# Decays of a bidirectional state-space scan: one minimum over both directions, or each direction by itself

## The chip, the cores and the metric

The kernel runs on one core of one Trainium2 chip. The metric is the device time of one execution in microseconds (us).

## The reference

The program is one layer of a bidirectional encoder trunk in float32 on 256 tokens of width 2048: a Mamba-2 scan in both directions, a 4-head cross-attention into 256 memory tokens, a gated feed-forward block with a convolution, and norms between them. What matters here is the scan. Its 64 heads of 64 features lie in 8 groups of 8 heads; a group shares one B and one C with 128 states. Time is cut into two chunks of 128 tokens. For one direction, with `cum` the running sum of `dt * A` (A is negative):

```
seg = exp(where(tril, cum[l] - cum[m], -inf))
cb  = C[l] . B[m]
y_diag[l] = sum over m of  cb[l,m] * seg[l,m] * dt[m] * x[m]
```

The backward direction is the same on flipped tokens, with `dt`, A and `cum` of its own, and both results are added. So a token pair (l, m) with m before l takes the forward decay and weight, a pair with m after l the backward one, and the diagonal takes both.

## The kernel before, in words

All matrix products with weights are made of float32 split in two parts: ACT copies a raw weight tile to `w_hi` (L106), DVE subtracts to get `w_lo` (L107), and PE multiplies hi by hi, hi by lo and lo by hi (L152, L153, L154 in `gemm_feat`, 24 matmuls to a weight tile of 128x1024 in the scan stage, 8 of each line). Raw tiles have a ring of 5 buffers (loaded by SP, L115), `w_hi` and `w_lo` a ring of 4 each.

The scan stage goes over 8 groups. For group g the program first writes down the projection of group g+1 (`project`: the products for x, then for B and C, each with the convolution and Silu), then the gate of group g (`project_z`), then `scan_group(g)`. Tile's planner places these instructions on the engines at build time, each engine's list in a fixed order, so the matmuls of the next projection stand between the steps of a group's scan.

The setup ahead of it (L296 to L356) computes `dt`, its transpose `dt_tok` (tokens in partitions), the running sums `cumT` for both directions, which go to `cum_d` in DRAM (L334), and `ncum_tok`, the negated running sums with tokens in partitions (L346). Exp, Ln and Silu need a table load on ACT when the function before was of another table.

`scan_group` takes both chunks c in turn. `r` (L423, one buffer, 128x2048) gets from `cum_d` the running sums of the group's 8 heads in both directions, sent to all 128 partitions (L424, 1 MB). `cb` holds C.B twice, masked for the forward and for the backward triangle (L428). Then:

- for each head: ACT adds the head's negated forward sum to the forward `r` (L435), DVE adds the negated backward sum to the backward `r` and takes the minimum of both (L436). One of the two is negative and the other positive off the diagonal, so the minimum is the right decay's exponent on either side;
- one Exp over all 8 heads (L438);
- for each head: ACT scales the backward `cb` by the backward `dt` (L441), DVE adds the forward `cb` times the forward `dt` (L442);
- DVE multiplies both (L444) to `t2`, and PE multiplies `t2` with x (L453). DVE adds the skip term and the part from the other chunk (L456 to L460), and in the end the gate (L464).

After the second chunk the same buffer `r` is loaded for the next group. SP works its list in order: L424 waits until `r` has been read, with the raw weight loads behind it.

Of the kernel before, what the change touches and what calls it, by code (L numbers as in the profile page):

```python
# [10 lines left out]
AF = mybir.ActivationFunctionType  # L11
ALU = mybir.AluOpType
AX = mybir.AxisListType

P = 128
T = 256
# [20 lines left out]
def kernel(  # L37
# [15 lines left out]
    nc = tc.nc  # L53

    const = ctx.enter_context(tc.tile_pool(name="const", bufs=1))
# [7 lines left out]
    def sb(pool, shape, tag, dtype=F32, **kw):  # L63
        return pool.tile(shape, dtype, tag=tag, name=tag, **kw)
# [178 lines left out]
    with tc.tile_pool(name="xin", bufs=1) as xin:  # L243
        xt = [sb(xin, [P, D], f"x{tt}") for tt in range(2)]
        dt_w = []
        for q4 in range(4):
            if q4 == 2:
                dt_w.append(load_raw(w_in_v, 0, [(10240, P)]))
            for tt in range(2):
                nc.sync.dma_start(out=xt[tt][:, q4 * 512:(q4 + 1) * 512],  # L250
                                    in_=x[tt * P:(tt + 1) * P, q4 * 512:(q4 + 1) * 512])
        ss = sb(xin, [P, 2, 4], "x_ss")
        for u in range(4):
            stage = sb(xin, [P, 4, T], "x_stage", bufs=2)
            for jj in range(2):
                ps = psum_m()
# [20 lines left out]
        ps = psum_m()  # L277
# [4 lines left out]
        nc.vector.tensor_copy(out=r_mix, in_=ps[:, :T])  # L282

    dt_tok = sb(const, [P, 2, P], "dt_tok")
    ncum_tok = sb(const, [P, 2, P], "ncum_tok")
    dx_tok = sb(const, [P, 2, 64], "dx_tok")
    units_y = []

    with tc.tile_pool(name="ssd", bufs=1) as ssd:
# [53 lines left out]
        ps = psum_m()  # L343
        for c in range(2):
            nc.tensor.transpose(out=ps[:, c * P:(c + 1) * P], in_=cumT[:, c, :], identity=ident)
        nc.vector.tensor_scalar(out=ncum_tok.rearrange("p c h -> p (c h)"), in0=ps[:, :T], scalar1=-1.0,  # L346
                                scalar2=None, op0=ALU.mult)

        ecum = pieces[10][:, :P]
        for c in range(2):  # L350
# [42 lines left out]
        def scan_group(g, xs, bc, sz):  # L393
            hs = slice(g * 8, (g + 1) * 8)
            er = sb(ssd, [P, 2, 4, P], "er")
            for q in range(2):
                for d in range(2):
                    nc.sync.dma_start(out=er[q * 64:(q + 1) * 64, d], in_=ecum_v[g, q, d].partition_broadcast(64))

            xs_tok = sb(ssd, [P, 2, 512], "xs_tok")  # L400
            xsd = sb(ssd, [P, 2, 512], "xsd")
            for c in range(2):
                ps = psum_m()
                for j in range(4):
                    nc.tensor.transpose(out=ps[:, j * P:(j + 1) * P], in_=xs[:, j, c * P:(c + 1) * P], identity=ident)  # L405
                nc.scalar.copy(out=xs_tok[:, c, :], in_=ps)
                nc.vector.tensor_tensor(out=xsd[:, c, :].rearrange("p (h f) -> p h f", f=64),
                                        in0=ps.rearrange("p (h f) -> p h f", f=64),
                                        in1=dx_tok[:, c, hs].unsqueeze(2).broadcast_to([P, 8, 64]), op=ALU.mult)
            b_tok = sb(ssd, [P, 2, P], "b_tok")  # L410
            ps = psum_m()
            for c in range(2):
                nc.tensor.transpose(out=ps[:, c * P:(c + 1) * P], in_=bc[:, 0, c * P:(c + 1) * P], identity=ident)
            nc.scalar.copy(out=b_tok.rearrange("p c n -> p (c n)"), in_=ps[:, :T])

            st = sb(ssd, [P, 2, 512], "st")
            for c in range(2):
                ps = psum_m()
                nc.tensor.matmul(ps, b_tok[:, c, :], xsd[:, c, :], start=True, stop=True)  # L419
                nc.scalar.copy(out=st[:, c, :], in_=ps)  # L420
            for c in range(2):
                cl = slice(c * P, (c + 1) * P)
                r = sb(ssd, [P, 2, 8, P], "r")  # L423
                nc.sync.dma_start(out=r, in_=cum_v[c, g].partition_broadcast(P))  # L424
                ps_cb = psum_m()
                nc.tensor.matmul(ps_cb[:, :P], bc[:, 0, cl], bc[:, 1, cl], start=True, stop=True)
                cb = sb(ssd, [P, 2, P], "cb")
                nc.vector.tensor_tensor(out=cb, in0=ps_cb[:, :P].unsqueeze(1).broadcast_to([P, 2, P]), in1=tri, op=ALU.mult)  # L428


                t1 = r[:, 0]
                t2 = sb(ssd, [P, 8, P], "t2", bufs=2)
                for h in range(8):
                    hf, hb = g * 8 + h, 64 + g * 8 + h
                    nc.scalar.activation(out=t1[:, h, :], in_=t1[:, h, :], func=AF.Identity, bias=ncum_tok[:, c, hf:hf + 1])  # L435
                    nc.vector.scalar_tensor_tensor(out=t1[:, h, :], in0=r[:, 1, h, :], scalar=ncum_tok[:, c, hb:hb + 1],  # L436
                                                   in1=t1[:, h, :], op0=ALU.add, op1=ALU.min)
                nc.scalar.activation(out=t1, in_=t1, func=AF.Exp)  # L438
                for h in range(8):
                    hf, hb = g * 8 + h, 64 + g * 8 + h  # L440
                    nc.scalar.activation(out=t2[:, h, :], in_=cb[:, 1, :], func=AF.Copy, scale=dt_tok[:, c, hb:hb + 1])  # L441
                    nc.vector.scalar_tensor_tensor(out=t2[:, h, :], in0=cb[:, 0, :], scalar=dt_tok[:, c, hf:hf + 1],  # L442
                                                   in1=t2[:, h, :], op0=ALU.mult, op1=ALU.add)
                nc.vector.tensor_tensor(out=t2, in0=t2, in1=t1, op=ALU.mult)  # L444

                ps_o = psum_m()
                for j in range(4):
                    nc.tensor.matmul(ps_o[:, j * P:(j + 1) * P], st[:, 1 - c, j * P:(j + 1) * P], bc[:, 1, cl],  # L448
                                     start=(j == 0), stop=(j == 3), skip_group_check=True)
                ps_y = psum_m()  # L450
                for h in range(8):
                    dst = ps_y[(h % 2) * 64:(h % 2 + 1) * 64, (h // 2) * P:(h // 2 + 1) * P]
                    nc.tensor.matmul(dst, xs_tok[:, c, h * 64:(h + 1) * 64], t2[:, h, :],  # L453
                                     start=(h < 2), stop=(h >= 6), skip_group_check=True)
                for j in range(4):
                    nc.vector.scalar_tensor_tensor(out=xs[:, j, cl], in0=xs[:, j, cl], scalar=pcol("dskip", g * 4 + j),  # L456
                                                   in1=ps_y[:, j * P:(j + 1) * P], op0=ALU.mult, op1=ALU.add)
                yo = er[:, 1 - c]
                nc.vector.tensor_tensor(out=yo, in0=ps_o.rearrange("p (j l) -> p j l", l=P), in1=yo, op=ALU.mult)
                nc.vector.tensor_tensor(out=xs[:, :, cl], in0=xs[:, :, cl], in1=yo, op=ALU.add)  # L460
            unit = new_unit()
            for b in range(2):
                bs = slice(2 * b, 2 * b + 2)
                nc.vector.tensor_tensor(out=xs[:, bs, :], in0=xs[:, bs, :], in1=sz[:, bs, :], op=ALU.mult)  # L464
                add_square(ssd, acc_y, xs[:, bs, :], g == 0 and b == 0)
                for j in range(2 * b, 2 * b + 2):
                    split_scaled(unit, j, xs[:, j, :], pcol("g_ssd", g * 4 + j))
            units_y.append(unit)
# [306 lines left out]
```

## Time and profile before

| what | us |
|---|---|
| median of 3 runs | 1862.79 (1862.3 to 1864.23) |
| the profiled execution | 1863.24 |
| its span, first to last instruction | 1861.5 |
| PE busy (matmuls) | 1842.3 |
| DVE busy | 1264.2 |
| ACT busy | 1018.2 |

PE is the matrix engine, PEld its weight loads, DVE the vector engine, ACT the scalar engine, SP the queue that issues the transfers. Busy time of PE is a union of matmuls whose ends are modelled. An instruction's duration can overlap the next one's on the same engine, so the pace of a row of equal instructions is read from their starts.

### The profile page before, as it was taken

The page shows a single profiled execution, that of the slowest core. Times are in us where ns is not written, and L with a number is a line of the kernel's source. Part 1 is how long each engine was busy: PE and PEld are TensorE (multiplying, and loading weights), DVE is VectorE, ACT ScalarE, POOL GpSimd, SP SyncE. Part 2 cuts the span into 40 slices and gives each one's busy share as a digit, 9 for nine tenths or more (in the row PEclk, how much of TensorE's full clock was granted, in tenths as well). Part 3 has the DMA queues.
Part 4 walks back from the last instruction along what each step waited for, and adds up shares of the span by engine and source line. Part 5 has one row for each costly group of instructions (what it writes and reads, how often), then busy time and mean ns, then how long its engine had stood idle before and what let it go on. Part 6 is the DMA issues. An engine that isn't in the chain of part 4 may idle for free.

```text
span 1861.5 us, 29854 instructions
## 1 busy us (share of the span) xinstructions
PE 1842.3 (99%) x11821; PEld 1663.5 (89%) x11821; DVE 1264.2 (68%) x1792; ACT 1018.2 (55%) x1454; POOL 2.3 (0%) x11
## 2 busy tenths in 40 slices
PE   8999999999999999999999999999999999999997
PEld 8999999999999988888888888888888888888886
DVE  6878888988887756655555667666664456666654
ACT  6667667766775645444444455555553345555443
POOL 0000000000000000000000000000000000000000
PEclk9999999999999999999999999999999999999999
DMA  8667666766766765655655556566666666666563
GB/s 289 198 203 214 199 189 201 219 197 201 215 182 205 244 197 182 184 177 170 176 176 181 164 187 206 179 189 188 191 191 192 193 192 188 185 187 187 190 193 114
DMA packets 289708, 358.94 MB, mean 193 GB/s; under 512 B 11616, under 2 KB 210656, under 8 KB 289056
## 3 DMA queue, kind: packets, MB, share of 16 engines
q1 hardware_dynamic: 289488, 356.76, 62.3%
q8 instruction: 92, 1.51, 0.3%
q14 instruction: 48, 0.39, 0.1%
q0 software_dynamic: 80, 0.28, 0.1%
HBM read 352.60 MB, written 4.39 MB: 192 GB/s over the span
## 4 chain that ended last, share of the span: by engine, by line
PE 99%; DMA 0%; DVE 0%; ACT 0%; SPq 0%; issue 0%; DVEq 0%
PE psg L169 30%; PE psg L171 16%; PE psg L154 10%; PE psg L153 10%; PE psg L152 10%; PE psm L194 6%; PE psm L193 6%; PE psm L195 6%; PE psm L453 1%; PE psm L448 1%; PE psm L419 1%; PE psm L589 0%; PE psm L591 0%; PE psm L590 0%; DMA x<-in_x_dram 0%; PE psm L405 0%
## 5 line engine op out<-in xcount | busy, mean ns | idle before, releaser
L107 DVE TENSOR_TENSOR w_lo<-raw,w_hi 128x1024 fp32r<-128x1024 f32 x618 | 753.7, 1223 | 499.3 <-ACT w_hi L106 497.1
L106 ACT CAST w_hi<-raw 128x1024 fp32r<-128x1024 f32 x618 | 645.7, 1049 | 684.0 <-PE psg L169 314.5
L169 PE MATMUL psg<-unit,w_hi 128*128 128x512 f32 x2432 | 853.3, 396 | 0.0
L171 PE MATMUL psg<-unit,w_lo 128*128 128x256 f32 x2432 | 683.4, 281 | 0.0
L169 PEld LDWEIGHTS psg<-unit,w_hi 128*128 128x128 f32 x2432 | 456.3, 188 | 106.0
L171 PEld LDWEIGHTS psg<-unit,w_lo 128*128 128x128 f32 x2432 | 460.7, 189 | 0.2
L154 PE MATMUL psg<-unit,w_lo 128*128 128x256 f32 x1552 | 444.8, 287 | 0.1
L152 PE MATMUL psg<-unit,w_hi 128*128 128x256 f32 x1552 | 442.4, 285 | 0.0
L153 PE MATMUL psg<-unit,w_hi 128*128 128x256 f32 x1552 | 441.6, 285 | 0.0
L154 PEld LDWEIGHTS psg<-unit,w_lo 128*128 128x128 f32 x1552 | 298.6, 192 | 3.4 <-issue 3.1
L152 PEld LDWEIGHTS psg<-unit,w_hi 128*128 128x128 f32 x1552 | 298.7, 193 | 1.7 <-issue 1.7
L153 PEld LDWEIGHTS psg<-unit,w_hi 128*128 128x128 f32 x1552 | 298.7, 193 | 0.3 <-issue 0.2
L195 PE MATMUL psm<-w_hi,unit 128*128 128x512 f32 x480 | 187.0, 390 | 0.0
L194 PE MATMUL psm<-w_lo,unit 128*128 128x512 f32 x480 | 187.0, 390 | 0.0
L193 PE MATMUL psm<-w_hi,unit 128*128 128x512 f32 x480 | 186.9, 389 | 0.0
L193 PEld LDWEIGHTS psm<-w_hi,unit 128*128 128x128 f32 x480 | 90.1, 188 | 18.9
L195 PEld LDWEIGHTS psm<-w_hi,unit 128*128 128x128 f32 x480 | 90.1, 188 | 18.8
L194 PEld LDWEIGHTS psm<-w_lo,unit 128*128 128x128 f32 x480 | 90.1, 188 | 18.4
L435 ACT ACTIVATE r<-r,ncum_tok 128x128 f32<-128x128 f32 x128 | 39.4, 390 | 57.5 <-DMA r<-cum_d 57.5
L436 DVE SCALAR_TENSOR_TENSOR r<-r,ncum_tok 128x128 f32<-128x128 f32 x128 | 37.0, 347 | 16.7 <-ACT r L435 16.7
L441 ACT ACTIVATE t<-cb,dt_tok 128x128 f32<-128x128 f32 x128 | 39.1, 389 | 0.7 <-DVE cb L428 0.2
L442 DVE SCALAR_TENSOR_TENSOR t<-cb,dt_tok,t 128x128 f32<-128x128 f32 x128 | 36.5, 349 | 3.3 <-ACT t L441 3.3
(222 smaller groups left out, 1076.4 us busy)
## 6 DMA issues: line engine op xcount, KB each, us to landing
raw<-in_w_up_dram SPq DMA_DIRECT2D x176, 512.0 KB, 3.7
raw<-in_w_in_dram SPq DMA_DIRECT2D x130, 512.0 KB, 4.6
raw<-in_w_down_dram SPq DMA_DIRECT2D x88, 512.0 KB, 3.8
raw<-in_w_out_dram SPq DMA_DIRECT2D x64, 512.0 KB, 4.2
raw<-in_wkv_dram SPq DMA_DIRECT2D x64, 512.0 KB, 3.8
raw<-in_w_in_dram SPq DMA_DIRECT2D x64, 256.0 KB, 4.4
r<-cum_d SPq DMA_DIRECT2D x16, 1024.0 KB, 6.3
raw<-in_wq_dram SPq DMA_DIRECT2D x32, 512.0 KB, 3.5
```

What stands on the lines that cost most here:

```text
L106: nc.scalar.copy(out=hi, in_=src)
L107: nc.vector.tensor_tensor(out=lo, in0=src, in1=hi.bitcast(F32), op=ALU.subtract)
L152: nc.tensor.matmul(dst, wh, uh, start=first, stop=False, skip_group_check=True)
L153: nc.tensor.matmul(dst, wh, ul, start=False, stop=False, skip_group_check=True)
L154: nc.tensor.matmul(dst, wl, uh, start=False, stop=last, skip_group_check=True)
L169: nc.tensor.matmul(ps[:, ft, :], hi[:, kk, fs], unit[2][:, kt % 4].rearrange("p s t -> p (s t)"), start=(kt == 0), stop=False, skip_group_ ...
L171: nc.tensor.matmul(ps[:, ft, :T], lo[:, kk, fs], unit[0][:, kt % 4, :], start=False, stop=(kt == nk - 1), skip_group_check=True)
L193: nc.tensor.matmul(banks[tt], uh, hi[:, kk, :], start=(kt == 0), stop=False)
L194: nc.tensor.matmul(banks[tt], uh, lo[:, kk, :], start=False, stop=False)
L195: nc.tensor.matmul(banks[tt], ul, hi[:, kk, :], start=False, stop=(kt == nk - 1))
L435: nc.scalar.activation(out=t1[:, h, :], in_=t1[:, h, :], func=AF.Identity, bias=ncum_tok[:, c, hf:hf + 1])
L441: nc.scalar.activation(out=t2[:, h, :], in_=cb[:, 1, :], func=AF.Copy, scale=dt_tok[:, c, hb:hb + 1])
```

## The change

The exponent is formed for each direction by itself: `off_tok` = ln dt - cum, and ln dt joins the exponent. Each is bounded above by ln dt (`ldt_tok`), so that the wrong triangle cannot overflow; the mask in `cb` then sets it to zero. Both steps are one tensor_scalar with two operands per partition, on DVE, for each head and direction. Exp runs once for each direction, each is multiplied with its own masked `cb`, and the two are added.

```diff
     dt_tok = sb(const, [P, 2, P], "dt_tok")
-    ncum_tok = sb(const, [P, 2, P], "ncum_tok")
+    ldt_tok = sb(const, [P, 2, P], "ldt_tok")
+    off_tok = sb(const, [P, 2, P], "off_tok")
...
-        nc.vector.tensor_scalar(out=ncum_tok.rearrange("p c h -> p (c h)"), in0=ps[:, :T], scalar1=-1.0,
-                                scalar2=None, op0=ALU.mult)
+        nc.vector.tensor_scalar(out=ldt_tok, in0=dt_tok, scalar1=1e-37, scalar2=None, op0=ALU.max)
+        nc.scalar.activation(out=ldt_tok, in_=ldt_tok, func=AF.Ln)
+        nc.vector.tensor_tensor(out=off_tok.rearrange("p c h -> p (c h)"), in0=ldt_tok.rearrange("p c h -> p (c h)"),
+                                in1=ps[:, :T], op=ALU.subtract)
...
-                t1 = r[:, 0]
+                for h in range(8):
+                    for d in range(2):
+                        hd = d * 64 + g * 8 + h
+                        nc.vector.tensor_scalar(out=r[:, d, h, :], in0=r[:, d, h, :], scalar1=off_tok[:, c, hd:hd + 1],
+                                                scalar2=ldt_tok[:, c, hd:hd + 1], op0=ALU.add, op1=ALU.min)
                 t2 = sb(ssd, [P, 8, P], "t2", bufs=2)
-                for h in range(8):
-                    hf, hb = g * 8 + h, 64 + g * 8 + h
-                    nc.scalar.activation(out=t1[:, h, :], in_=t1[:, h, :], func=AF.Identity, bias=ncum_tok[:, c, hf:hf + 1])
-                    nc.vector.scalar_tensor_tensor(out=t1[:, h, :], in0=r[:, 1, h, :], scalar=ncum_tok[:, c, hb:hb + 1],
-                                                   in1=t1[:, h, :], op0=ALU.add, op1=ALU.min)
-                nc.scalar.activation(out=t1, in_=t1, func=AF.Exp)
-                for h in range(8):
-                    hf, hb = g * 8 + h, 64 + g * 8 + h
-                    nc.scalar.activation(out=t2[:, h, :], in_=cb[:, 1, :], func=AF.Copy, scale=dt_tok[:, c, hb:hb + 1])
-                    nc.vector.scalar_tensor_tensor(out=t2[:, h, :], in0=cb[:, 0, :], scalar=dt_tok[:, c, hf:hf + 1],
-                                                   in1=t2[:, h, :], op0=ALU.mult, op1=ALU.add)
-                nc.vector.tensor_tensor(out=t2, in0=t2, in1=t1, op=ALU.mult)
+                for d in range(2):
+                    nc.scalar.activation(out=r[:, d], in_=r[:, d], func=AF.Exp)
+                for d in range(2):
+                    nc.vector.tensor_tensor(out=r[:, d], in0=r[:, d],
+                                            in1=cb[:, d:d + 1, :].broadcast_to([P, 8, P]), op=ALU.mult)
+                nc.vector.tensor_tensor(out=t2, in0=r[:, 0], in1=r[:, 1], op=ALU.add)
```

## Rows read from the trace of the kernel before

**Rows 1.** The page, part 1: busy us (share of the span) xinstructions, by engine.

```profile
PE 1842.3 (99%) x11821; PEld 1663.5 (89%) x11821; DVE 1264.2 (68%) x1792; ACT 1018.2 (55%) x1454; POOL 2.3 (0%) x11
```

**Rows 2.** Waits of PE: line, releaser, us in total, times, longest.

```profile
PE psm L260 <- DMA x<-in_x_dram: 6.3, 5, 3.8
PE psm L453 <- DVE t L444: 1.5, 1, 1.5
```

**Rows 3.** Windows: length, busy PE, PEld, DVE, ACT, POOL, clock, DMA share, GB/s.

```profile
375.89:440.92 65.03, 65.03 (x549) 63.46 (x547) 55.06 (x101) 44.86 (x79) 0.00 (x0) 1.00 0.68 204
...
50.00:75.00 25.00, 24.90 (x206) 24.62 (x205) 21.46 (x40) 17.23 (x21) 0.00 (x0) 1.00 0.67 189
```

**Rows 4.** Groups by line: removed or doubled instructions; busy us, mean ns, idle before.

```profile
L435 ACT ACTIVATE r<-r,ncum_tok 128x128 f32<-128x128 f32 x128 | 39.4, 390 | 57.5 <-DMA r<-cum_d 57.5
L441 ACT ACTIVATE t<-cb,dt_tok 128x128 f32<-128x128 f32 x128 | 39.1, 389 | 0.7 <-DVE cb L428 0.2
L436 DVE SCALAR_TENSOR_TENSOR r<-r,ncum_tok 128x128 f32<-128x128 f32 x128 | 37.0, 347 | 16.7 <-ACT r L435 16.7
L442 DVE SCALAR_TENSOR_TENSOR t<-cb,dt_tok,t 128x128 f32<-128x128 f32 x128 | 36.5, 349 | 3.3 <-ACT t L441 3.3
L444 DVE TENSOR_TENSOR t<-t,r 128x1024 f32<-128x1024 f32 x16 | 19.6, 1224 | 9.4 <-ACT r L438 9.2
L438 ACT ACTIVATE r<-r 128x1024 f32<-128x1024 f32 x16 | 16.9, 1059 | 0.1
```

**Rows 5.** Groups by line: instructions nearest to the added ones.

```profile
L280 DVE TENSOR_SCALAR r_b<-ones,r_x 128x128 f32<-128x128 f32 x2 | 0.5, 282 | 0.1
L298 DVE TENSOR_SCALAR r<-r,par 128x256 f32<-128x256 f32 x1 | 0.3, 347 | 0.0
L304 DVE TENSOR_SCALAR r<-r 128x256 f32<-128x256 f32 x1 | 0.3, 294 | 0.8 <-ACT r L301 0.8
...
L306 ACT ACT_TABLE_LOAD x1 | 1.3, 1283 | 0.0
...
L306 ACT ACTIVATE r<-r 128x256 f32<-128x256 f32 x1 | 0.4, 418 | 0.0
```

**Rows 6.** Timeline of DVE in one period: start us, us, instruction, idle before.

```profile
387.32 1.23 DVE L444 TENSOR_TENSOR t<-t,r 128x1024 f32<-128x1024 f32 x1
388.46 0.68 DVE L459 TENSOR_TENSOR er<-psm,er 128x512 f32<-128x512 f32 x1
...
398.15 2.18 DVE L442 SCALAR_TENSOR_TENSOR t<-cb,dt_tok,t 128x128 f32<-128x128 f32 x8
...
402.98 1.22 DVE L444 TENSOR_TENSOR t<-t,r 128x1024 f32<-128x1024 f32 x1 [1.14 <-ACT r L438]
...
411.42 0.94 DVE L436 SCALAR_TENSOR_TENSOR r<-r,ncum_tok 128x128 f32<-128x128 f32 x3 [1.57 <-ACT r L435]
412.27 0.68 DVE L460 TENSOR_TENSOR xs<-xs,er 128x512 f32<-128x512 f32 x1
...
414.19 1.29 DVE L464 TENSOR_TENSOR xs<-xs,sz 128x512 f32<-128x512 f32 x2
415.39 2.36 DVE L107 TENSOR_TENSOR w_lo<-raw,w_hi 128x1024 fp32r<-128x1024 f32 x2
```

**Rows 7.** Timeline of ACT in the same period: the two waits for `r`.

```profile
394.85 2.45 ACT L435 ACTIVATE r<-r,ncum_tok 128x128 f32<-128x128 f32 x8 [2.53 <-DMA r<-cum_d]
...
410.98 2.45 ACT L435 ACTIVATE r<-r,ncum_tok 128x128 f32<-128x128 f32 x8 [4.82 <-DMA r<-cum_d]
```

**Rows 8.** Timeline of PE in the same period: the use of `t2` and of one w_lo.

```profile
406.03 1.09 PE L453 MATMUL psm<-t,xs_tok 128*64 128x128 f32 x16
...
417.84 0.28 PE L153 MATMUL psg<-unit,w_hi 128*128 128x256 f32 x1
417.96 0.28 PE L154 MATMUL psg<-unit,w_lo 128*128 128x256 f32 x1
```

**Rows 9.** The page, part 6: DMA issues, KB each, us to landing.

```profile
r<-cum_d SPq DMA_DIRECT2D x16, 1024.0 KB, 6.3
```

## The prediction

> **What bounds the kernel now.** I began with the page's busy times: PE is busy 1842.3 of 1861.5 us, DVE 68%, ACT 55% [rows 1]. The whole span says little of a stage, so next came the waits of PE by line: it waits 6.3 us for the first input and 1.5 us, once, for the product `t2` of the scan (L444); no other wait is listed [rows 2]. All that a lighter scan can give back to a PE that issues at its present pace is therefore 1.5 us. Then the windows: cut where the transposes of one group begin and those of the next, the scan stage repeats every 65.03 us, and in the period shown PE is busy 65.03 of them at full clock, DVE 55.06 and ACT 44.86 [rows 3]. PE is fed by the w_hi and w_lo tiles that ACT and DVE make from raw weights, and the same two engines do the scan. So the change touches two engines that are not the bound; the question is only whether DVE, with 9.97 us idle per period, still delivers w_lo tiles and `t2` in time.
>
> How close it is now is read from the timelines of one period. `r` for the second chunk has landed when ACT starts L435 at 394.85; `t2` is done at 402.98 + 1.22 = 404.20, and PE begins the matmuls on it (L453) at 406.03, 1.8 us later [rows 6 to 8]. The tightest w_lo tile of the period is the first of the pair that starts at 415.39. It is done at 416.6, and by counting 8 L154 matmuls to a tile, PE first reads it at 417.96: a margin of 1.3 us [rows 6, 8]. Before it ACT stood 4.82 us waiting for `r`, which held back the w_hi casts behind it, and DVE did none but scan work from 411.42 on [rows 6, 7].
>
> **The change part by part.** Per chunk, 16 chunks in all:
>
> ACT loses 8 Identity (L435) and 8 Copy (L441), eight of L435 taking 2.45 us in a row [rows 7] and those of L441 lasting as long one by one, and gains a second Exp of 1.06 us [rows 4]. That is 4.9 - 1.06 = 3.8 us less per chunk, 7.7 per period. ACT then works some 37 of 65 us. This is off the path and shortens nothing by itself.
>
> DVE loses 16 scalar_tensor_tensor (L436, L442). Their duration is 347 and 349 ns [rows 4], but eight in a row take 2.18 us, so one occupies 0.27 [rows 6]: 16 x 0.27 = 4.3 us. The one product of 1.22 us occupies 1.14 (387.32 to 388.46) [rows 6]. Together 5.5. It gains 16 tensor_scalar of 128x128 and three tensor_tensor of 128x1024, 3 x 1.14 = 3.4 us. No row shows a tensor_scalar with two column operands. The nearest is L280, 128x128 with one column, 282 ns [rows 5]. In a row such instructions lie about 0.08 closer than they last (0.35 against 0.27 above), hence 0.20 from below. One column costs 347 - 294 = 53 ns (L298 against L304) [rows 5], so a second gives 0.25, which I take; from above 0.35, the scalar_tensor_tensor's duration with no overlap. So 16 x 0.25 + 3.4 = 7.4 us per chunk (6.6 to 9.0), 1.9 more than before (1.1 to 3.5), 3.8 per period (2.2 to 7.0). DVE's idle time falls from 9.97 to 6.2 us (3.0 to 7.8): it still has room.
> [...]
>
> The path from `r` to `t2` in one chunk: now 404.20 - 394.85 = 9.4 us. After: 16 tensor_scalar 4.0; a table load of 1.28 [rows 5] if it stands behind the wait; Exp 1.06 and the second, closer, about 0.97; beside the second Exp the first product; then the second product 1.14 and the sum 1.22. That is 9.7 us (8.9 to 11.3), 0.3 later than now (0.5 earlier to 1.9 later), against the margin of 1.8. The first chunk of a group has its `r` long before; it needs three operations of 1.14 behind `cb` where it needed eight of L442 and one product (2.2 + 1.14), so nothing changes there.
>
> SP: `r` is one buffer, so the load of the next `r` (L424) waits for the sum instead of L444, 0.3 us later by the above, and the raw loads queued behind it on SP move with it. Landing takes 6.3 us [rows 9] as before. I cost it at nothing while w_lo tiles keep their margin.
>
> What stands behind the new wait: now ACT waits for `r`, and w_hi casts queue behind it. Afterwards DVE waits for `r`, and w_lo tiles, the conv steps and the gate queue behind it. DVE's wait is covered by the ring of four tiles, about 2.88 us of PE each (24 matmuls that start 0.12 us apart [rows 8]), and ACT is free, so the casts are done while DVE stands. Taking the tight place again: `r` lands 0.3 later, at 411.3; 16 tensor_scalar make it 415.3, L460 and the pair of L464 take about 0.6 + 1.2 if they stay in front, and the tile of 1.22 is done at 418.3. Without those three in front it is done at 416.5, with the tensor_scalar behind the tile earlier still. So here the margin of 1.3 us ends between -0.4 and well above 1.3. The order of work on each engine is laid down at build time by a planner whose costs no row shows; I choose to let the tiles come in time, because the next group's decays are needed only with its own `cb`, which comes after a whole further gate projection, and can yield to them.
>
> Setup: one tensor_scalar and one Ln on 128x256, 0.29 and 0.42, and one or two table loads of 1.28 (L306, the Ln there, has one of its own) [rows 5]. In 50 to 75 us ACT is busy 17.23 and DVE 21.46 of 25 [rows 3]. They lie beside the first projection's matmuls; without that cover they would cost at most 0.29 + 0.42 + 2.57 = 3.3 us. I take 0.
>
> Last chunk: the 1.5 us wait [rows 2] has no cover, so the path's 0.3 goes through in full (-0.5 to 1.9).
>
> **Sum.** The profiled execution took 1863.24 us (span 1861.5 and 1.7 around it), 0.45 over the median of 1862.79. 1863.24 + 0 + 0.3 = 1863.5; against the median 1863.1. A measurement here can tell about 0.2%, 3.7 us, from no change, so the forecast is no change, from 1859.1 to 1866.5.
>
> **Rivals.**
> Slower by DVE's wait for `r`: the 16 tensor_scalar stand ahead of two w_lo tiles in DVE's order, so a late `r` starves PE. For it: DVE is already the busier helper, and the margin is 1.3 us. Against it: ACT stood 4.82 us at that place, its freed time removes just that wait from the w_hi side, and DVE's idle time stays positive. It decides once the tile comes more than 1.3 us later than now. Price: 0.4 us per period with 0.25 per tensor_scalar (above), and 16 x 0.10 = 1.6 more with 0.35, so 0.4 to 2.0, times 7 periods that have a next group: 3 to 14 us; 1866 to 1877, in the middle 1872. Chance 0.33, with everything that lets `t2` come later than its 1.8 us counted in.
>
> Faster because PE's record hides stalls: matmul ends are modelled, and PE could be slowed without showing idle time. The weight loads are busy 63.46 of 65.03 us in the period [rows 3]; were all of the 1.57 us a stall behind scan work, 8 x 1.57 + 1.5 = 14 us would come back, 1849. Against it: in the rows shown matmuls start an even 0.12 us apart [rows 8], while ACT and DVE are anything but even there [rows 6, 7]. Chance 0.07. [...]
>
> That the change doesn't do what it says, the tensor_scalar being as dear as the instructions they replace, is the upper price of 0.35 and lies inside the first rival.
>
> **How the numbers follow.** No change 0.60 (own range 1860.5 to 1866), slower 0.33, faster 0.07. The range starts at 1860, just below the no-change case, and leaves the faster case out; it ends at 1876, near the dear end of the slower case, and leaves out about 0.1 above that.
>
> **What would show it.** Right: the scan period stays at 65.0 us with PE busy throughout; DVE near 59 us and ACT near 37 per period; tensor_scalar 0.28 to 0.34 us each; the waits for `r` on DVE instead of ACT. Wrong: waits of PE on w_lo or on the sum that make more than 3.7 us together, or a period below 64.6 us.

## The result and the profile after

The changed kernel takes 1877.74 us in the median of 4 runs (1875.44 to 1880.27); the kernel before, run beside it, 1863.51 (4 runs). The ratio is 1.0077, with a 95% interval of 1.0064 to 1.0089: slower. No change had been forecast, 1863.1 us; the measured time is also 1.7 us above the top of the range.

The profiled execution took 1880.27 us, its span 1878.6, which is 17.1 us more than before. The page of the changed kernel, part 1 (busy us, share of the span, instructions), is read first, against [rows 1]:

```profile
PE 1845.8 (98%) x11821; PEld 1665.9 (89%) x11821; DVE 1294.6 (69%) x1825; ACT 961.5 (51%) x1216; POOL 2.3 (0%) x11
```

PE has the same 11821 matmuls. Its idle time is 1878.6 - 1845.8 = 32.8 us where it was 1861.5 - 1842.3 = 19.2: 13.6 us more of standing still. The other 3.5 us are matmuls that took longer. ACT lost 57 us of work and DVE gained 30, and DVE still has 31% of the span idle.

Where PE stands is told by its waits (line, releaser, us in total, times, longest), against [rows 2]:

```profile
PE psg L154 <- DVE w_lo L107: 7.3, 7, 2.1
PE psm L260 <- DMA x<-in_x_dram: 5.9, 3, 3.8
PE psg L169 <- DVE res_t L499: 3.0, 1, 3.0
PE psg L152 <- DVE sz L390: 2.0, 1, 2.0
PE psg L152 <- DVE cv_s L366: 1.9, 1, 1.9
PE psg L152 <- ACT xs L377: 0.9, 1, 0.9
```

The single wait of before for `t2` is gone. In its place stand 7.3 us for w_lo tiles, 1.9 and 2.0 for DVE steps that read PSUM (where PE puts its sums) and so free it, 0.9 for such a step on ACT, and 3.0 at the first matmul of the wide output projection behind the scan (L169). All but the last lie in the scan: 12.1 us. Less the 1.5 of before, these five rows make 13.6 us, the added idle time.

The matmuls that took longer are found in windows (length, busy PE, PEld, DVE, ACT, POOL, clock, DMA share, GB/s) cut behind the pauses. The first row is an undisturbed stretch, the last one follows a pause that left no trace:

```profile
180.00:250.00 70.00, 70.00 (x591) 68.43 (x590) 62.89 (x111) 41.94 (x55) 0.00 (x0) 1.00 0.69 203
...
165.20:168.61 3.41, 3.41 (x18) 3.41 (x17) 3.41 (x5) 3.41 (x8) 0.00 (x0) 0.51 0.80 196
...
318.76:322.17 3.41, 3.41 (x19) 3.41 (x18) 3.41 (x6) 3.35 (x8) 0.00 (x0) 0.50 0.62 199
...
660.09:663.50 3.41, 3.41 (x13) 2.93 (x12) 0.18 (x1) 0.00 (x0) 0.00 (x0) 0.50 0.94 403
...
455.63:459.04 3.41, 3.41 (x28) 3.41 (x29) 2.87 (x5) 3.41 (x8) 0.00 (x0) 1.00 0.46 159
```

In three stretches of 3.41 us the granted clock is half of full (0.50, in the first window 0.51), and PE does 18 and 19 matmuls of the scan, of which the last row holds 28 at full clock, and 13 of the longer ones behind it. By estimate each costs 3.41 / 2 = 1.7 us, 5.1 together. They follow pauses that ended at 164.65 (1.72 us long), 318.06 (1.85) and 659.64 (3.01). The page's 3.5 us of longer matmuls are 1.6 less than these 5.1, because a stretch behind the scan ran a little faster (told under "What stays open").

Now the engine that made PE wait. The timeline of DVE in the changed kernel (start, us, instruction, idle before) at the longest of its gaps, against [rows 6]. It is the load of `r` for the first chunk of a group, the same step that the prediction argued about, one group earlier:

```profile
356.66 3.52 DVE L107 TENSOR_TENSOR w_lo<-raw,w_hi 128x1024 fp32r<-128x1024 f32 x3
360.06 1.15 DVE L459 SCALAR_TENSOR_TENSOR xs<-xs,par,psm 128x128 f32<-128x128 f32 x4
365.54 0.86 DVE L439 TENSOR_SCALAR r<-r,off_tok,ldt_tok 128x128 f32<-128x128 f32 x3 [4.33 <-DMA r<-cum_d]
366.31 0.69 DVE L463 TENSOR_TENSOR xs<-xs,er 128x512 f32<-128x512 f32 x1
366.92 3.42 DVE L439 TENSOR_SCALAR r<-r,off_tok,ldt_tok 128x128 f32<-128x128 f32 x13
370.24 1.30 DVE L467 TENSOR_TENSOR xs<-xs,sz 128x512 f32<-128x512 f32 x2
371.44 2.37 DVE L107 TENSOR_TENSOR w_lo<-raw,w_hi 128x1024 fp32r<-128x1024 f32 x2
...
433.41 2.14 DVE L439 TENSOR_SCALAR r<-r,off_tok,ldt_tok 128x128 f32<-128x128 f32 x8 [1.33 <-DMA r<-cum_d]
```

The last w_lo tile ahead of the wait is done at 360.2. DVE then stands 4.33 us for `r`, all 16 tensor_scalar and both gate steps follow, and the next tile begins at 371.44: 11.3 us without a new w_lo tile. With the prediction's estimate of 2.88 us of PE for a tile, the ring of four holds 4 x 2.88 = 11.5 us of PE's work, if it is full when the gap begins. It was not: PE runs 28 matmuls of L154, three and a half tiles, before it has to wait for the first new one:

```profile
372.73 0.39 PE L154 MATMUL psg<-unit,w_lo 128*128 128x256 f32 x1 [1.51 <-DVE w_lo L107]
```

The last row of DVE's timeline is the very load that the prediction took. There 14 of the 16 tensor_scalar and the gate steps also stand ahead of the next tile, but DVE waits only 1.33 us, the gap is 6.1, and PE does not pause.

From the timelines I took this gap, last tile's end to next tile's start around the first operation on `r`, at each of the 15 loads of `r` after the first. Its mean is 7.1 us before (longest 10.7) and 8.9 after (longest 11.3).

Part of the gap is `r` itself. The groups by line (busy us, mean ns, idle before), against [rows 4], then the changed kernel's part 6 of the page (KB, us to landing), against [rows 9]:

```profile
L439 DVE TENSOR_SCALAR r<-r,off_tok,ldt_tok 128x128 f32<-128x128 f32 x256 | 68.8, 349 | 39.5 <-DMA r<-cum_d 39.5
...
L443 ACT ACTIVATE r<-r 128x1024 f32<-128x1024 f32 x32 | 32.2, 1052 | 30.9 <-DVE r L439 30.9
...
r<-cum_d SPq DMA_DIRECT2D x16, 1024.0 KB, 8.0
```

The wait for `r` is now DVE's, 39.5 us in all, and ACT waits 30.9 us behind DVE. The load takes 8.0 us to land where it took 6.3. The waits of SP bear on it; first the row of before, then that of after (SPq is SP's queue):

```profile
SPq L424 <- DVE t L444: 52.3, 15, 6.0
```

```profile
SPq L428 <- DVE t L447: 18.8, 12, 4.0
```

Before, SP stood 52.3 us at the load until `r` had been read, and in that time the raw weight loads ahead of it came in. By the trace, its loads of `r` went out with no raw load in flight (5.8 to 6.2 us to land) or with one (6.1 to 6.9), the first and the last load of the scan apart. Afterwards SP waits only 18.8 us there, and of the 15 loads after the first seven go out with two raw loads in flight (6.7 to 8.6 us), six with one (5.9 to 8.7) and two with none (5.9 and 6.2). So more loads overlap others, but one load in flight goes with 6.1 to 6.9 before and up to 8.7 after: the number alone does not give the landing, and what does stays open.

The last row of PE's waits lies behind the scan. PE's timeline of the changed kernel there:

```profile
654.60 1.47 PE L531 MATMUL psm<-ident,mem 128*128 128x128 f32 x12
655.82 0.36 PE L154 MATMUL psg<-unit,w_lo 128*128 128x256 f32 x1
656.03 0.60 PE L531 MATMUL psm<-ident,mem 128*128 128x128 f32 x4
659.64 0.47 PE L169 MATMUL psg<-unit,w_hi 128*128 128x512 f32 x1 [3.01 <-DVE res_t L499]
```

At that place DVE's timeline, of the kernel after and then of the kernel before:

```profile
656.28 1.23 DVE L107 TENSOR_TENSOR w_lo<-raw,w_hi 128x1024 fp32r<-128x1024 f32 x1 [1.53 <-ACT unit L101]
657.42 0.87 DVE L102 SCALAR_TENSOR_TENSOR unit<-psm,par,unit 128x256 fp32r<-128x256 f32 x2
658.21 1.28 DVE L499 TENSOR_TENSOR res_t<-psg,r_ssd 128x512 f32<-128x512 f32 x2
```

```profile
630.31 1.23 DVE L107 TENSOR_TENSOR w_lo<-raw,w_hi 128x1024 fp32r<-128x1024 f32 x1 [1.53 <-ACT unit L101]
631.45 0.87 DVE L102 SCALAR_TENSOR_TENSOR unit<-psm,par,unit 128x256 fp32r<-128x256 f32 x2
632.24 1.27 DVE L496 TENSOR_TENSOR res_t<-psg,r_ssd 128x512 f32<-128x512 f32 x2
```

DVE does the same things at the same pace in both: a tile, the split of two transposes (L102), and the reading of PE's sums out of PSUM (L499, L496 before), for which L169 waits. What differs is PE. In the kernel after one matmul of the projection stands between the last two groups of transposes (L531) and none behind them, so PE has nothing to do for 3.0 us. Before, the last transposes are at 631.37 and the first L169 at 642.00, and the 85 matmuls between them cover the same work. Nothing in the diff touches this stage: the planner, given other instructions on DVE and ACT, laid down another order for PE.

### The profile page after: what moved, and what is told of

Read it like the earlier page. It is cut to its first block, busy times and chain, and to the rows that moved or that the text cites. A ratio compares the mean times of both kernels' runs of the same rounds, so it can differ in the third digit from the quotient of the medians.

```text
span 1878.6 us, 29646 instructions
## 1 busy us (share of the span) xinstructions
PE 1845.8 (98%) x11821; PEld 1665.9 (89%) x11821; DVE 1294.6 (69%) x1825; ACT 961.5 (51%) x1216; POOL 2.3 (0%) x11
## 4 chain that ended last, share of the span: by engine, by line
PE 67%; DVE 0%; issue 0%; ACT 0%; DVEq 0%
PE psg L169 30%; PE psg L171 15%; PE psm L195 6%; PE psm L193 6%; PE psm L194 6%; PE psg L154 1%; PE psg L152 1%; PE psg L153 1%; PE psm L592 0%; PE psm L594 0%; PE psm L593 0%; PE psm L692 0%; PE psm L531 0%; PE psm L620 0%; DVE h_tok L731 0%
## 5 line engine op out<-in xcount | busy, mean ns | idle before, releaser
L169 PE MATMUL psg<-unit,w_hi 128*128 128x512 f32 x2432 | 852.4, 395 | 3.0 <-DVE res_t L499 3.0
L171 PE MATMUL psg<-unit,w_lo 128*128 128x256 f32 x2432 | 681.6, 280 | 0.0
L169 PEld LDWEIGHTS psg<-unit,w_hi 128*128 128x128 f32 x2432 | 456.6, 188 | 108.4 <-ACT unit L101 3.2
L171 PEld LDWEIGHTS psg<-unit,w_lo 128*128 128x128 f32 x2432 | 459.9, 189 | 0.2
L154 PE MATMUL psg<-unit,w_lo 128*128 128x256 f32 x1552 | 445.0, 287 | 7.3 <-DVE w_lo L107 7.3
L154 PEld LDWEIGHTS psg<-unit,w_lo 128*128 128x128 f32 x1552 | 299.3, 193 | 10.8 <-DVE w_lo L107 8.8
L439 DVE TENSOR_SCALAR r<-r,off_tok,ldt_tok 128x128 f32<-128x128 f32 x256 | 68.8, 349 | 39.5 <-DMA r<-cum_d 39.5
L443 ACT ACTIVATE r<-r 128x1024 f32<-128x1024 f32 x32 | 32.2, 1052 | 30.9 <-DVE r L439 30.9
L445 DVE TENSOR_TENSOR r<-r,cb 128x1024 f32<-128x1024 f32 x32 | 38.0, 1229 | 0.2
L178 DVE TENSOR_TENSOR f_s<-psg,f_s 128x512 f32<-128x512 f32 x44 | 30.1, 684 | 0.0
```

What stands on the lines that cost most here:

```text
L154: nc.tensor.matmul(dst, wl, uh, start=False, stop=last, skip_group_check=True)
L169: nc.tensor.matmul(ps[:, ft, :], hi[:, kk, fs], unit[2][:, kt % 4].rearrange("p s t -> p (s t)"), start=(kt == 0), stop=False, skip_group_ ...
L171: nc.tensor.matmul(ps[:, ft, :T], lo[:, kk, fs], unit[0][:, kt % 4, :], start=False, stop=(kt == nk - 1), skip_group_check=True)
L439: nc.vector.tensor_scalar(out=r[:, d, h, :], in0=r[:, d, h, :], scalar1=off_tok[:, c, hd:hd + 1], scalar2=ldt_tok[:, c, hd:hd + 1], op0=AL ...
L445: nc.vector.tensor_tensor(out=r[:, d], in0=r[:, d], in1=cb[:, d:d + 1, :].broadcast_to([P, 8, P]), op=ALU.mult)
```

## The experiments

The theories: **W**, DVE's wait for the one buffer `r` holds up w_lo tiles; **D**, DVE simply has more work; **C**, the path from `r` to `t2` is too long; **P**, the planner's other order costs PE its cover; **B**, formed later, a wait costs only together with a burst of work behind it on the same engine. The notes on each run give its ratio to the kernel before with the 95% interval.

**A second buffer for `r`, in the kernel after.** The sum is written into `r` itself, which makes the room.

```diff
-                r = sb(ssd, [P, 2, 8, P], "r")
+                r = sb(ssd, [P, 2, 8, P], "r", bufs=2)
...
-                t2 = sb(ssd, [P, 8, P], "t2", bufs=2)
+                t2 = r[:, 0]
```

> The changed kernel with two buffers for r; the sum is written into r's forward half, which makes room for the second buffer. DVE does the same instructions. Theory W (DVE stands for r ahead of w_lo tiles): the 39.5 us that L439 waits for r fall below 8, PE's pauses of about 12 us in the scan go, 1861 to 1866 us. Theory D (DVE's added work alone, 1.9 us per chunk): DVE works as long as before in each period, so the time stays at 1874 to 1880. Theory P (the planner's new order of PE, whose one pause of 3.0 us after the memory transposes and the half clock behind it are part of the loss): whatever the scan does, about 5 us of the loss stay, 1867 to 1870.

Measured: 1864.94 us (11 runs), ratio 1.0016 (1.0008 to 1.0025). Its group of tensor_scalar, a window of the scan, and the one wait of PE it lists besides that for the first input:

```profile
L439 DVE TENSOR_SCALAR r<-r,off_tok,ldt_tok 128x128 f32<-128x128 f32 x256 | 70.3, 342 | 15.9 <-DMA r<-cum_d 15.8
...
180.00:250.00 70.00, 70.00 (x581) 67.35 (x581) 64.44 (x111) 39.74 (x53) 0.00 (x0) 1.00 0.67 197
...
PE psg L154 <- DVE w_lo L107: 1.4, 2, 1.2
```

DVE does the same 256 instructions and is as busy as in the kernel after (64.44 of 70 us against 62.89), yet PE waits 1.4 us in the scan instead of 12.1. So D alone is worth about the 0.16% that is left, and the loss goes with W's wait, though this fell from 39.5 us to 15.8 and not below 8. The pause at L169 is gone too, with no half clock in the scan stage: the planner's order changed again, so P's 5 us did not stay.

**The same second buffer in the kernel before.**

```diff
-                r = sb(ssd, [P, 2, 8, P], "r")
+                r = sb(ssd, [P, 2, 8, P], "r", bufs=2)
...
-                t2 = sb(ssd, [P, 8, P], "t2", bufs=2)
+                t2 = r[:, 1]
```

> The kernel before with two buffers for r (t2 is written into r's backward half, which is free after the minimum). W and D alike: ACT's 57.5 us of waits for r fall below 15, but PE waited only 1.5 us for the scan, so the time stays within 0.2% of the kernel before, 1860 to 1864. A gain of more than 4 us would say that waits for r cost PE something that its own waits did not show.

Measured: 1861.72 us (11 runs), ratio 0.9994 (0.9985 to 1.0003). ACT's waits for `r` fell only to 39.1 us, where less than 15 was expected. The buffer is worth nothing measurable where the wait did no harm; it repairs, it doesn't improve.

**Half of the tensor_scalar.** The backward direction gets neither its offset nor its bound; DVE's work is then about that of before (59.06 of 70 us busy from 180 to 250, 58.85 before).

```diff
-                    for d in range(2):
+                    for d in range(1):
```

> The changed kernel without the eight tensor_scalar of the backward direction, which leaves the backward exponent without its offset and bound. DVE's work per chunk falls by 8 x 0.256 = 2.0 us, to what it was before the change. W: the wait for r stays where it is and DVE reaches it no later, so it stays at 35 us or more and the time at 1869 or more. D: the time goes back to 1861 to 1866.

Measured: 1871.2 us (5 runs), ratio 1.0051 (1.0037 to 1.0064). In the groups, and among ACT's waits:

```profile
L439 DVE TENSOR_SCALAR r<-r,off_tok,ldt_tok 128x128 f32<-128x128 f32 x128 | 35.6, 342 | 54.8 <-DMA r<-cum_d 54.8
...
ACT L443 <- DMA r<-cum_d: 46.7, 8, 8.1
```

With DVE's work back, two thirds of the loss (0.51 of 0.77%) stay. The wait is even longer, 54.8 us, and the burst behind it half as long. The run is not a clean removal of DVE's work: the backward Exp now waits for `r` itself, 46.7 us ahead of its table load and 35.6 ahead of the Exp, which holds up w_hi casts, and the pause at L169 (P) is gone too.

**Only the wait, in the kernel before.** DVE copies one column of `r` ahead of L435, so it waits for `r` as in the kernel after.

```diff
+                nc.vector.tensor_copy(out=r[:, 0, 0, 0:1], in_=r[:, 0, 0, 0:1])
```

> The kernel before with one DVE copy of a single column of r ahead of L435, so that DVE waits for r and has 16 x about 0.06 us more work, 1 us in all. W: DVE stands 2 to 4 us in each chunk ahead of w_lo tiles, PE pauses 3 to 12 us more, 1866 to 1875. D: nothing to speak of, 1862 to 1865.

Measured: 1863.74 us (11 runs), ratio 1.0004 (0.9996 to 1.0013). W in its plain form missed. DVE's timeline:

```profile
414.36 0.15 DVE L432 COPY r<-r 128x1 f32<-128x1 f32 x1 [4.40 <-DMA r<-cum_d]
414.46 1.22 DVE L107 TENSOR_TENSOR w_lo<-raw,w_hi 128x1024 fp32r<-128x1024 f32 x1
```

DVE stands 4.40 us, as long as in the kernel after, but the copy takes 0.15 and a w_lo tile follows at once. PE's waits for w_lo tiles make 1.0 us in all, 0.6 at most at once, so waits of that length alone were all but covered by the ring here. The mean gap between tiles is 5.8 us here. Few of its waits are that long, though: 22.7 us in all, 6.2 of them at the first load.

**The offsets on ACT.** The bound is a constant 40, set by two wide tensor_scalar for each chunk; 16 Identity on ACT add the offsets, one direction after the other.

```diff
-                        nc.vector.tensor_scalar(out=r[:, d, h, :], in0=r[:, d, h, :], scalar1=off_tok[:, c, hd:hd + 1],
-                                                scalar2=ldt_tok[:, c, hd:hd + 1], op0=ALU.add, op1=ALU.min)
+                        nc.scalar.activation(out=r[:, d, h, :], in_=r[:, d, h, :], func=AF.Identity, bias=off_tok[:, c, hd:hd + 1])
+                    nc.vector.tensor_scalar(out=r[:, d], in0=r[:, d], scalar1=40.0, scalar2=None, op0=ALU.min)
```

> The changed kernel with the offset added on ACT (16 Identity of 128x128 with a bias per partition) and one bound of 40 for a whole direction on DVE (two tensor_scalar of 128x1024) in place of the 16 tensor_scalar; each direction still by itself, r with one buffer. ACT waits for r again, and DVE's work per chunk is 2 x about 0.6 + 3.4 = 4.6 us, less than the 5.5 before the change. W (DVE stands for r with a burst of work behind it, ahead of tiles) and D (added DVE work): 1861 to 1865. If what costs the time is the chain from r to t2 being longer (theory C: 16 x 0.3 + bound + two Exp + three products, about 11 us against 9.4), PE pauses at the scan's matmuls, 1867 to 1876.

Measured: 1888.11 us (4 runs), ratio 1.0141 (1.0127 to 1.0155): slower than the kernel after, where W and D had expected the loss to go, and above C's 1867 to 1876 too. ACT's timeline, and the waits of PE:

```profile
338.22 4.80 ACT L439 ACTIVATE r<-r,off_tok 128x128 f32<-128x128 f32 x16 [3.32 <-DMA r<-cum_d]
342.92 1.04 ACT L106 CAST w_hi<-raw 128x1024 fp32r<-128x1024 f32 x1
...
PE psg L154 <- DVE w_lo L107: 6.4, 12, 0.8
...
PE psm L423 <- ACT b_tok L418: 4.2, 3, 3.6
PE psg L152 <- ACT w_hi L106: 3.4, 4, 1.6
PE psm L456 <- DVE t L447: 3.2, 5, 1.2
```

The pattern moved with the work: ACT stands for `r` and a burst of 16 in 4.80 us follows, now ahead of w_hi casts, from which the w_lo tiles are made. A wait with a burst of 16 behind it cost time on either engine (ratio 1.0077 on DVE, 1.0141 on ACT), as B has it. The 3.2 us for `t` (L447) are C's part, which the kernel after does not have, so not all of this loss is B's.

**The same with two buffers.** The edit of the run before and that of the first run together.

```diff
+                r = sb(ssd, [P, 2, 8, P], "r", bufs=2)
...
+                        nc.scalar.activation(out=r[:, d, h, :], in_=r[:, d, h, :], func=AF.Identity, bias=off_tok[:, c, hd:hd + 1])
```

> The same with two buffers for r and the sum in r. W and D: 1860 to 1863, the least of all, as neither engine waits long nor has more work than before. C: 1862 to 1866, since the load no longer belongs to the chain.

Measured: 1863.1 us (11 runs), ratio 1.0002 (0.9993 to 1.001). That is 0.1 above what W and D gave and inside C's range. Again the second buffer takes the whole loss away.

**`r` in two transfers.** One for each direction, and the directions one after the other, so that DVE can begin on the first half.

```diff
-                nc.sync.dma_start(out=r, in_=cum_v[c, g].partition_broadcast(P))
+                for d in range(2):
+                    nc.sync.dma_start(out=r[:, d], in_=cum_v[c, g, d].partition_broadcast(P))
```

> The changed kernel with r loaded in two transfers, one for each direction, and the tensor_scalar of the forward direction first. The first eight can start when half of r is there, 2 to 3 us earlier. W: DVE's waits for r fall from 39.5 us to 10 to 25 and the time to 1866 to 1873. D: no change, 1874 to 1880.

Measured: 1872.56 us (5 runs), ratio 1.0054 (1.0041 to 1.0067). The time lies in W's range and its interval just touches that of the kernel after, but not by the means meant: DVE's wait for `r` did not fall to 10 to 25 us, it did not get shorter at all.

```profile
L440 DVE TENSOR_SCALAR r<-r,off_tok,ldt_tok x256: 333/342/355, 80.8 to 586.8; 128x128 f32<-128x128 f32 x128
...
  DMA r<-cum_d: 42.8, 15
```

The burst is cut in two, and the mean gap between tiles fell from 8.9 to 8.1 us. How much of a gain is due to that and how much to another order is not told apart.

**Memory tokens loaded by another queue.** To see whether the 3.0 us at L169 come from these loads or from PE's order.

```diff
-            nc.sync.dma_start(out=m, in_=mem[tt * P:(tt + 1) * P, :])
+            nc.gpsimd.dma_start(out=m, in_=mem[tt * P:(tt + 1) * P, :])
```

> The changed kernel with the two loads of the memory tokens issued by POOL instead of SP. The order on PE stays as it is but for six projection matmuls, which now follow the last memory transposes. P (of the loss about 6 us come from the pause behind those transposes, with no matmul left to cover it, and the half clock after it): 1 us less at most, 1874 to 1880, with the pause at the first matmul of the wide output projection still over 1.5 us. If the pause there is gone and the time under 1873, the loads were late and not the order.

Measured: 1880.05 us (5 runs), ratio 1.0101 (1.0084 to 1.0117). PE's order hardly changed, and a wait of PE and a window that starts half a microsecond before the wait ends repeat those of the kernel after:

```profile
PE psg L169 <- DVE res_t L499: 3.0, 1, 3.0
...
658.70:662.10 3.40, 2.93 (x9) 2.58 (x10) 1.10 (x3) 0.00 (x0) 0.00 (x0) 0.50 1.00 429
```

The run moved the loads hardly at all: POOL issues them at 625.6 and 626.1, SP did at 625.5 and 625.9. What clears them is the trace of the kernel after, where both had landed by 634.3 and the first transposes start at 643.86. Counted in PE's timelines, four kernels have no matmul of the projection behind the last transposes: the kernel after, the two with changed transfers (this one and the one before it), and the one with a changed ring below. Three of them wait 3.0 us at L169, the fourth 1.5. The other nine kernels have 13 to 133 matmuls there, and none waits more than 0.14 us. That agrees with P, though no run changed these matmuls alone.

**Only the burst, in the kernel before.** The forward offset goes from ACT to DVE.

```diff
-                    nc.scalar.activation(out=t1[:, h, :], in_=t1[:, h, :], func=AF.Identity, bias=ncum_tok[:, c, hf:hf + 1])
+                    nc.vector.tensor_scalar(out=t1[:, h, :], in0=t1[:, h, :], scalar1=ncum_tok[:, c, hf:hf + 1], scalar2=None, op0=ALU.add)
```

> The kernel before with its eight forward additions (L435) moved from ACT to DVE as tensor_scalar, and nothing else: the wait for r and a burst of 16 small operations stand on DVE, as in the changed kernel, without the directions by themselves. Theory B (wait and burst on one engine, together longer than the ring of four tiles covers): a gap between w_lo tiles of 9 us or more at each r, PE pauses of 6 us or more, 1868 to 1882. If the cost lay in the new exponents, the two Exp or the three products: 1862 to 1866.

Measured: 1861.73 us (11 runs), ratio 0.9993 (0.9984 to 1.0002). B's number missed, because B's condition wasn't met. The planner put the burst behind more w_lo tiles, so that `r` had nearly landed:

```profile
413.17 1.23 DVE L107 TENSOR_TENSOR w_lo<-raw,w_hi 128x1024 fp32r<-128x1024 f32 x1 [0.27 <-ACT w_hi L106]
...
415.33 1.66 DVE L435 TENSOR_SCALAR r<-r,ncum_tok 128x128 f32<-128x128 f32 x8 [0.34 <-DMA r<-cum_d]
```

DVE waits 18.6 us for `r` in all instead of 39.5. The run became the missing corner: a burst with little wait cost nothing measurable (ratio 0.9993). It speaks against D as well, with DVE busy 61.90 of 70 us from 180 to 250, nearly as in the kernel after (62.89).

**A ring of five weight tiles.** Paid for with a raw ring of three; in the kernel after, and as a control in the kernel before.

```diff
-    ring_raw = ctx.enter_context(tc.tile_pool(name="ring_raw", bufs=5))
-    ring = ctx.enter_context(tc.tile_pool(name="ring", bufs=4))
+    ring_raw = ctx.enter_context(tc.tile_pool(name="ring_raw", bufs=3))
+    ring = ctx.enter_context(tc.tile_pool(name="ring", bufs=5))
```

> The changed kernel with five w_hi and w_lo tiles in the ring instead of four; the room comes from the raw ring, three instead of five. B: one tile more covers 2.9 us more, so that DVE may stand 35 us or more for r and PE's pauses in the scan still fall below 4 us in all; 1861 to 1869 (the upper end if the pause behind the memory transposes stays). If DVE's waits are not covered by the ring (D, or a longer chain to t2): 1873 to 1880. Fewer raw tiles may cost something by themselves; the run beside it tells.

> The kernel before with the same rings, five and three. It has nothing to gain but PE's 1.5 us and shows what fewer raw tiles cost: 1860 to 1866 if nothing; over 1868 would make the run beside it hard to read.

Measured: after 1885.78 us (5 runs), ratio 1.0115 (1.0096 to 1.0133); before 1864.31 (11 runs), 1.0007 (0.9998 to 1.0015). The first missed. In the waits of its PE:

```profile
PE psg L152 <- DVE cv_s L366: 6.6, 3, 2.6
...
PE psg L154 <- DVE w_lo L107: 3.1, 2, 2.2
PE psg L152 <- DVE sz L390: 2.4, 1, 2.4
```

More cover did lower the wait for w_lo, 7.3 to 3.1 us. But PE then waited more where DVE reads PSUM (1.9 and 2.0 in the kernel after, 6.6 and 2.4 here), which fits a backlog of DVE that shows at the next thing it owes PE. As the raw ring shrank as well and the order changed, this run is no clean test of the cover alone.

The runs side by side, by what follows the wait for `r`:

| kernel | engine that waits | us waited | burst behind it | mean w_lo gap, us | ratio |
|---|---|---|---|---|---|
| before | ACT | 57.5 | 8 | 7.1 | 1 |
| before with a one-column copy | DVE | 22.7 | one copy | 5.8 | 1.0004 |
| before, offset on DVE | DVE | 18.6 | 8, little wait | 7.4 | 0.9993 |
| after, half of the tensor_scalar | DVE | 54.8 | 8 | 8.2 | 1.0051 |
| after, two transfers | DVE | 42.8 | 8 and 8 | 8.1 | 1.0054 |
| after | DVE | 39.5 | 16 | 8.9 | 1.0077 |
| after, offsets on ACT | ACT | 79.6 | 16 | 8.7 | 1.0141 |
| after, two buffers | DVE | 15.8 | 16, little wait | 5.1 | 1.0016 |
| after, offsets on ACT, two buffers | ACT | 13.8 | 16, little wait | 3.8 | 1.0002 |

In the kernels with a change, a wait without a burst and a burst without much of a wait cost 0.16% at most. The two together cost 0.5 to 1.4%, and the time is lost where the mean gap passes about 8 us. Two rows limit this. The kernel before has a long wait and a burst of 8 on ACT at no loss, while 8 on DVE behind a like wait go with 0.51%, so the engine is not indifferent. And with the offset on DVE single gaps of up to 10.2 us passed without a pause of PE: the fill of the ring counts as well as the gap.

**What stays open.** The planner orders each kernel anew, so no run takes the wait away with every order kept. The split of the 17 us is therefore read from the trace and not from a run: in the scan 12.1 - 1.5 us of pauses and two half-clock stretches, 14 us; at L169 3.0 and one such stretch, 4.7; and 1.6 back elsewhere. The starts of the same matmuls in both traces bear this out: the kernel after is 13.9 us late at its last L154, 17.6 at its first L169, 19.2 ten L169 later, and 16.6 at its last L169. The 2.6 us come back in the stage of L169 and L171, where a pair of them starts every 0.347 us on average instead of 0.353 (the 40th to the 200th pair), with PE busy throughout in both. No version here beats the kernel before measurably: the two best, the second buffer and the offset on DVE, reach 0.9994 and 0.9993 with 1 inside both intervals.

## Why the prediction was wrong

By its own steps:

**What bounds the kernel.** Right: PE is still busy 98% of the span, and everything lost is PE standing or running at half clock.

**ACT's work.** Right in kind. Scaled from the window of 70 us to 65, ACT is busy 41.94 x 65 / 70 = 39 us, where 37 was written, and it shortened nothing.

**DVE's work.** Right. A tensor_scalar lasts 349 ns, a little above the 280 to 340 given, but 13 in a row take 3.42 us, which is (3.42 - 0.35) / 12 = 0.256 apart; 0.25 was taken. DVE works 62.89 x 65 / 70 = 58.4 us in 65, where 59 was written. By the two-buffer run this added work, forecast as harmless, is worth about 0.16%.

**The path from `r` to `t2`, and the last chunk.** Mis-sized: from the first operation on `r` to the end of `t2` the second chunks of the groups take 13.5 us in the mean (12.2 to 14.5), where 9.4 was read and 9.7 (8.9 to 11.3) forecast. Four or five w_lo tiles and other work of DVE stand between its steps, which the sum left out. It cost PE no wait of its own: PE, held up elsewhere, no longer outruns `t2`, and the 1.5 us of the last chunk are gone. What it did to the next load is told under SP.

**SP and the landing.** Wrong: "Landing takes 6.3 us [rows 9] as before. I cost it at nothing while w_lo tiles keep their margin." The load takes 8.0 us in the median, mostly with one or two raw loads in flight at its issue in place of none or one. The condition in that sentence failed, and its price, 1.7 us more at the head of a gap whose margin was 1.3, was not worked out. The issue was mis-sized too. In both traces each load of `r` after the first goes out 0.03 us behind the end of the operation that reads `r` last (L444, L447). So the path of 13.5 us sends the load for the next group some 4 us later after the chunk's first operation on `r`, where 0.3 was forecast. How much of DVE's wait for `r` comes from the later issue, and how much from the longer landing, no run separates.

**What stands behind the new wait.** This is the step that failed: "I choose to let the tiles come in time, because the next group's decays are needed only with its own `cb`, which comes after a whole further gate projection, and can yield to them." The planner did not let them yield. One group ahead of the place argued, all 16 tensor_scalar and the gate steps of L463 and L467 stand between the wait of 4.33 us and the pair of tiles, and the pair starts 11.3 us after the last tile's end, where the same gap was 6.8 in the kernel before. At the place argued itself the order is nearly the same, but the wait was short and the tile came in time; over all 15 loads the gap averages 8.9 us against 7.1. PE's seven waits for w_lo, 7.3 us, are what the step had put at nothing. The paragraph also let the ring's four tiles cover "DVE's wait", as if the wait and the work behind it were separate. The runs show that on DVE either alone was covered (ratios 1.0004 and 0.9993) and both in a row were not (1.0077).

**The setup.** Right: its Ln (L349) and table load lie beside matmuls, and PE's first pause behind those for the first input comes at 86.13, in the scan, 0.23 us long.

**The rivals.** The first one came true in its mechanism, with 0.33 where it should have been the likeliest. Its price of 3 to 14 us was mis-sized. It counted only the tile's lateness, up to 2.0 us for each of 7 periods, which is near the scan's pauses, 12.1 - 1.5 = 10.6 us measured; in part by luck, as only 7.3 of them are waits for tiles and the rest are for steps that free PSUM, which the price did not name. It left out the half clock behind pauses (3 x 1.7 us) and the cover PE lost at L169 (3.0 us). Those put the time above the range. The second rival, hidden stalls, found nothing in the scan: no run came out below the kernel before by more than its interval. Its idea is not empty, though: the 0.347 against 0.353 us of L169 is time that PE's busy record did not show as open. Of the 1.57 us in each period in which the weight loads are not busy [rows 3], no run here gave any back measurably, which does not show that none could.

**What would show it.** Both signs were named ahead: tensor_scalar and waits as forecast, and, for wrong, PE waits on w_lo of more than 3.7 us. The trace has 7.3.

## What to carry to other kernels

A wait that moves to another engine is to be priced with the work queued directly behind it: wait plus burst, against what the ring holds ahead of the critical engine, and not the engine's idle time, which was still 7.1 of 70 us in the scan here. Where the wait is for a single buffer, a second copy (made room for by writing a result in place) removed the pattern here on either engine (ratio 1.0077 to 1.0016 on DVE, 1.0141 to 1.0002 on ACT). In a kernel ordered by a planner, a change on two helpers can also reorder the critical engine (3.0 us of standing at L169 here), so look for lost cover in stages that the diff doesn't touch, and leave room for it in the range.

## What the runs showed that was not expected

- TensorE drops to half clock after some pauses inside an otherwise full stretch: 3.41 us at a granted clock of 0.50 after pauses of 1.72, 1.85 and 3.01 us. Pauses of 2.02 and 2.10 us, which ended at 455.63 and 599.22, were followed by full clock. In the run with the memory tokens on another queue one of 1.86 us was followed by full clock and one of 2.54 by half. What tells them apart stayed open; the length alone does not.
- With no raw load in flight at its issue, the 1 MB load landed in 5.5 to 6.4 us in each of the seven kernels where I found that case. Loads in flight don't settle the rest alone: with two, it took 6.7 to 8.6 in the kernel after, but 6.0 once in the kernel after with two buffers.
- A tensor_scalar of 128x128 with two per-partition operands takes 349 ns and 0.256 us in a row. With one (L435 in the run that has only the burst) it takes 283 ns, and eight take 1.66 us, (1.66 - 0.28) / 7 = 0.20 each: so the second operand, with its minimum, costs about 0.06 us of DVE by estimate.
- Behind the scan, the pairs of L169 and L171 matmuls start 0.347 us apart (the 40th to the 200th) in the five kernels with at most 13 projection matmuls between the last memory transposes and the first L169, and 0.353 in the eight with 37 or more, PE busy throughout in all. Why was not looked into; it gives back part of what P costs.
